# Hybrid attention block on one core: new costs in the planner's table, one probability tile for two heads, and two small products in float32r with stacked parts

## The chip, the cores and the metric

The kernel runs on one core of a Trainium2 chip. The metric is the device time of one execution in microseconds. A core has five engines with instruction streams of their own: TensorE (PE, its weight loads are PEld), VectorE (DVE), ScalarE (ACT), GpSimd (POOL) and SyncE (SP, which only issues transfers here). Each engine works off its stream in order, and waits at an instruction until the semaphores that this instruction needs have come.

## The reference, cut to what matters

One decoder layer over 512 tokens of width 1024, all in float32.

```python
h = rmsnorm(x, norm1_w)
proj = h @ w_in        # columns: A (q, k, v), B (q, k, v, r, low-rank gate a), C (q, k, v)
y_a = dilated_attention(...)   # 6 heads, three (window, dilation) branches, T5 bias
y_b = gla(...)                 # 4 heads, gated linear attention
y_c = moba_attention(...)      # 6 heads, T5 bias; with 512 tokens: causal attention
x = x + concat(y_a, y_b, y_c) @ w_out
x = x + square(relu(rmsnorm(x, norm2_w) @ w_ff1)) @ w_ff2
return rmsnorm(x, final_norm_w)

# in gla, the product that the change touches:
log_a = log_sigmoid(a_lr @ w_a2 + b_a) / 16      # a_lr (512, 16), w_a2 (16, 128)
# in both attentions, the table that the change touches:
bias = rel_bias[rel_bucket(distance)]            # rel_bias (32 buckets, 12 heads)
```

## The kernel before, in words

The large products run in float32r, a reduced form of float32 that TensorE takes in one pass. So that nothing is lost, each factor is split in two parts: `hi`, the rounded value, and `lo`, what the rounding left over. A product is then three matmuls, hi·hi, lo·hi and hi·lo, and the splits are the main work of the other engines: ACT writes `wh` (hi of a weight tile), DVE writes `wl` (the tile less `wh`). Weights come by 512 KB transfers (`wraw`) that SP issues; sums of weight quarters, for a Strassen-like scheme with seven products instead of eight, are added by transfers that POOL issues or by DVE.

The order of the program on PE: the first projection (`first`, tiles `av`, `bq`, `bk`: eight steps of 18 matmuls, one per 128 rows of x); the q and k projections of head pairs 0 and 1 (`qkps`); the v projections (`vps`); `qkps` of pairs 2 to 5; the output projection (`ops`); and four times the two feed-forward products (`f1X`, `f1Y`, `f1Z`, then `f2X`, `f2Y`, `f2Z`). Into these streams of large matmuls small groups are dropped: the row sums `rsp`, the row scale spread over the partitions `rps`, the bias table `vt`, the gate product `zps` and the transposes before it `alps`, the gated attention's level products `lp`, the scores `sps`, transposes of probabilities `ptp`, products with values `po`, and the transposes `yps` before the feed-forward part.

No order is written out by hand. The kernel is a set of generators ("streams", `spawn`) that yield operations and waits. `Plan.run` keeps a clock for each engine and, for each tile, the time at which it is ready; at each step it issues the operation that could start first by these clocks. A cost for every operation stands in `Op.__init__` (lines 39 to 82), and `Plan.issue` adds for a transfer when it will have landed. So a number in that table moves instructions on every engine, and the built order is fixed once the kernel is compiled; the chip's own durations don't change it.

Names that the change and the steps below touch:

- `load_small` (line 622): POOL issues nine small loads: `cst` (identity and masks), `smask`, `hsel`, `rb` (the 32 bucket biases and two rows of ones, 34 rows by 12 heads), `bav`, `wa2` (16 by 128), the two halves of `oneh` (34 by 320, minus one at each distance's bucket), then `lmask` and `gw`. `rb`, `wa2` and `gw` lie in one tile, `misc`.
- `bias_table` (line 665): `vt` = `rb` times `oneh`, two float32 products, copied to `vals` and written to `tab` in DRAM, from where `nb` is read.
- `gla` (line 769): four columns `alr` on DVE, transposes `alps`, copy `alT`, the float32 product `zps` = `wa2` times `alT`, then the gate. `levels` makes seven pairs of factors `kq`; PE multiplies them two levels at a time into four banks (`lp`), and `copy_predicated` on DVE masks them into `attn`. The banks of a group of `lp` come free when its last four masked copies have run.
- `row_scale` (line 635): `rsp`, `ss`, `rstd`, the diagonal `diag` on DVE, then `rps` on PE and from it `R`.
- `attention` (line 951): for each head pair, four masked score groups; the probabilities of each head lie in `P0`, `P1`, `P2`.
- `y_out`, `y_parts`: the second norm, `yps`, `yf`, sums `ys`, and their parts `yp`, which `f1X`, `f1Y`, `f1Z` multiply.

In the profile every operation has line 133, the helper that issues it; in the changed kernel that line is 139. So instructions are told apart by their tiles.

## Time and profile before

| | |
|---|---|
| median of three runs | 565.54 us (564.97 to 566.04) |
| the profiled execution's own time | 565.34 us |
| its span, first to last instruction | 563.5 us |
| PE busy | 554.7 us, 98% of the span |
| PEld busy | 478.4 us, 85% |
| DVE busy | 480.4 us, 85% |
| ACT busy | 370.7 us, 66% |
| POOL busy | 69.7 us, 12% |
| granted TensorE clock | 0.998 |

The profiled execution's time holds the span and 1.8 us around it. A row of the timeline reads: start, duration, engine, line, operation, output<-inputs, shape, count, and in brackets the idle time before it and what ended that. Matmuls are pipelined: a 128x512 one has a duration of about 0.39 us, but the next begins 0.227 us after it. So what a matmul costs the engine is read from the distance of starts, not from its duration, and a busy PE can still lose time between starts.

### The profile page before, as it was taken

The page shows a single profiled execution, that of the slowest core. Times are in us where ns is not written, and L with a number is a line of the kernel's source. Part 1 is how long each engine was busy: PE and PEld are TensorE (multiplying, and loading weights), DVE is VectorE, ACT ScalarE, POOL GpSimd, SP SyncE. Part 2 cuts the span into 40 slices and gives each one's busy share as a digit, 9 for nine tenths or more (in the row PEclk, how much of TensorE's full clock was granted, in tenths as well). Part 3 has the DMA queues.
Part 4 walks back from the last instruction along what each step waited for, and adds up shares of the span by engine and source line. Part 5 has one row for each costly group of instructions (what it writes and reads, how often), then busy time and mean ns, then how long its engine had stood idle before and what let it go on. Part 6 is the DMA issues. An engine that isn't in the chain of part 4 may idle for free.

```text
span 563.5 us, 9460 instructions
## 1 busy us (share of the span) xinstructions
PE 554.7 (98%) x3513; PEld 478.4 (85%) x3513; DVE 480.4 (85%) x875; ACT 370.7 (66%) x658; POOL 69.7 (12%) x91
## 2 busy tenths in 40 slices
PE   9999999999999999999999999999999999999995
PEld 8978887867876768899987899988999888999884
DVE  7799999977868988999699995799957799867985
ACT  8664655884865775989766476855477654579553
POOL 5031110010000002110111010120020110011203
PEclk9999999999999999999999999999999999999999
DMA  8954685585124775992989429687378594395803
GB/s 317 393 123 123 128 217 124 161 335 103 38 43 127 242 150 115 271 272 60 274 212 204 163 64 278 201 151 204 113 158 283 121 201 158 95 220 113 150 12 137
DMA packets 29948, 96.58 MB, mean 171 GB/s; under 512 B 3648, under 2 KB 3690, under 8 KB 29904
## 3 DMA queue, kind: packets, MB, share of 16 engines
q0 software_dynamic: 9456, 33.53, 32.8%
q1 hardware_dynamic: 20160, 62.20, 31.5%
q8 instruction: 27, 0.44, 0.3%
q10 hardware_dynamic: 288, 0.27, 0.1%
q14 instruction: 17, 0.14, 0.1%
HBM read 93.86 MB, written 2.13 MB: 170 GB/s over the span
## 4 chain that ended last, share of the span: by engine, by line
PE 83%; DVE 11%; ACT 2%; issue 2%; DMA 2%; ACTq 0%; POOLq 0%
PE f2X L133 14%; PE f1X L133 13%; PE qkps L133 11%; PE f1Z L133 8%; PE ops L133 7%; PE f2Z L133 7%; PE f1Y L133 4%; PE vps L133 3%; PE f2Y L133 3%; DVE wl L133 3%; PE po L133 2%; PE ptp L133 2%; PE sps L133 2%; PE av L133 2%; DMA wraw<-in_w 2%
## 5 line engine op out<-in xcount | busy, mean ns | idle before, releaser
L133 DVE TENSOR_TENSOR wl<-wraw,wh 128x1024 fp32r<-128x1024 f32 (+2 forms) x174 | 192.0, 1111 | 38.2 <-ACT wh L133 37.2
L133 ACT ACTIVATE wh<-wraw 128x1024 fp32r<-128x1024 f32 (+2 forms) x173 | 164.7, 966 | 58.9 <-DMA wraw<-in_w 10.5
L133 PE MATMUL f1X<-yp,wh 128*128 128x256 f32 x512 | 92.7, 283 | 0.0
L133 PEld LDWEIGHTS f1X<-yp,wh 128*128 128x128 f32 x512 | 80.1, 192 | 0.3
L133 POOL DMA_DIRECT2D wraw<-in_w x46 | 40.8, 962 | 270.3 <-DVE wl L133 219.0
L133 PE MATMUL f1X<-yp,wl 128*128 128x256 f32 x256 | 72.5, 283 | 0.0
L133 PE MATMUL f2X<-wh,Al 128*128 128x512 f32 (+1 forms) x132 | 50.5, 383 | 0.0
L133 PE MATMUL f2X<-wh,Ah 128*128 128x512 f32 (+1 forms) x132 | 50.5, 383 | 0.0
L133 PE MATMUL f2X<-wl,Ah 128*128 128x512 f32 (+1 forms) x132 | 50.5, 383 | 0.0
L133 PEld LDWEIGHTS f1X<-yp,wl 128*128 128x128 f32 x256 | 49.1, 192 | 0.2 <-DVE wl L133 0.2
L133 PE MATMUL f1Z<-yp,wh 128*128 128x256 f32 x256 | 46.3, 283 | 0.0
L133 ACT ACTIVATE h<-h 128x512 f32<-128x512 f32 x56 | 34.7, 625 | 10.3 <-DVE h L133 9.8
L133 PE MATMUL qkps<-xh,wh 128*128 128x512 f32 x96 | 40.1, 417 | 0.0
L133 PEld LDWEIGHTS f1Z<-yp,wh 128*128 128x128 f32 x256 | 39.9, 192 | 0.0
L133 ACT ACTIVATE Ah<-h 128x512 fp32r<-128x512 f32 x40 | 24.0, 620 | 21.5 <-DVE h L133 21.5
L133 PE MATMUL qkps<-xh,wl 128*128 128x512 f32 x96 | 37.5, 391 | 0.0
L133 PE MATMUL qkps<-xl,wh 128*128 128x512 f32 x96 | 37.5, 390 | 0.0
L133 ACT ACTIVATE P<-P,mn 128x512 f32<-128x512 f32 (+3 forms) x48 | 26.6, 555 | 16.6 <-DVE mn L133 16.5
L133 PE MATMUL f1Z<-yp,wl 128*128 128x256 f32 x128 | 36.2, 283 | 0.0
L133 DVE TENSOR_TENSOR Al<-h,Ah 128x512 fp32r<-128x512 f32 x40 | 26.9, 687 | 3.2 <-ACT Ah L133 3.1
L133 PEld LDWEIGHTS f2X<-wl,Ah 128*128 128x128 f32 x132 | 24.8, 188 | 4.9
L133 PEld LDWEIGHTS f2X<-wh,Ah 128*128 128x128 f32 x132 | 24.8, 188 | 4.8
(266 smaller groups left out, 1223.9 us busy)
## 6 DMA issues: line engine op xcount, KB each, us to landing
wraw<-in_w SPq DMA_DIRECT2D x66, 512.0 KB, 5.2
wraw<-in_w POOLq DMA_DIRECT2D x46, 512.0 KB, 6.7
wraw<-in_wqk SPq DMA_DIRECT2D x12, 512.0 KB, 6.1
wraw<-in_wv SPq DMA_DIRECT2D x10, 512.0 KB, 8.6
wraw<-in_wv POOLq DMA_DIRECT2D x8, 512.0 KB, 6.0
wraw<-in_wo SPq DMA_DIRECT2D x8, 512.0 KB, 7.2
wraw<-in_wo POOLq DMA_DIRECT2D x8, 512.0 KB, 5.9
nb<-tab SPq DMA_DIRECT2D x12, 256.0 KB, 4.3
```

The lines of the kernel that those rows point to most:

```text
L133: getattr(getattr(self.nc, op.eng), op.method)(*op.args, **op.kw)
```

## The change

Four things are edited.

1. The planner's table: the 32-row `lp` matmul 0.031 to 0.0635 us; `tensor_tensor_scan` 1.13; `copy_predicated` 0.58 where the last dimension is one, else 0.33; 0.055 more for DVE operations with a per-partition scalar operand and for `scalar_tensor_tensor`. A plain load issued by POOL is now taken to land 3.0 us plus its size over 80 GB/s after its issue, and no longer goes through the clocks of the hardware queue.
2. The probabilities `P2` of the two heads of a pair share one 128x2x256 tile, one buffer instead of two.
3. The bias table: `oneh` and the weights are float32r now. The weights are stacked in 96 rows: rounded biases and the mask rows in rows 0 to 34, zeros, and in rows 64 to 95 the biases' rest; `oneh` repeats its bucket rows there. `rb` is loaded with 96 rows, and `stacked` makes the parts: ACT rounds into `stat`, DVE writes the rest.
4. The gate: `wa2` is loaded three times over (48 rows), with rows 32 to 47 turned into the rest; `alr` is split by three DVE operations into `al3` (rounded, rest, and the unrounded value, which the float32r write rounds), transposed as 48 columns, and `zps` is one float32r product.

```diff
@@ Op.__init__
-                self.cost = 0.031
+                self.cost = 0.0635
...
             self.cost = 0.075 + n * rate / 1000
+            if method == "tensor_tensor_scan":
+                self.cost = 1.13
+            elif method == "copy_predicated":
+                self.cost = 0.58 if args[0].shape[-1] == 1 else 0.33
+            elif any(a.shape[-1] == 1 and n > 4 for a in inner) or method == "scalar_tensor_tensor":
+                self.cost += 0.055
@@ Plan.issue
+            elif op.eng == "gpsimd":
+                end += 3.0 + op.size / 80e3
@@ tiles
-    rb, wa2, gw = misc[:, 0:128], misc[:, 128:256], misc[:, 256:512]
+    rb, wa2, gw = misc[:, 0:16], misc[:, 128:256], misc[:, 256:512]
+    stat = slot("stat", F32R)
+    rbs, wa2s = stat[:, 0:128], stat[:, 128:256]
-    oneh = [slot("oneh", shape=(128, 320)) for _ in range(2)]
-    alT = slot("alT", shape=(128, 512))
+    oneh = [slot("oneh", F32R, (128, 320)) for _ in range(2)]
+    alT = slot("alT", F32R, (128, 512))
@@ load_small
-        for t, d in ((cst, cst_d[:, 0:512]), (smask, cst_d[:, 512:1024]), (hsel, cst_d[:, 1024:1028]), (rb[:34, :12], rb_d),
-                     (bav, ba_d), (wa2[:16], wa2_d)):
+        for t, d in ((cst, cst_d[:, 0:512]), (smask, cst_d[:, 512:1024]), (hsel, cst_d[:, 1024:1028]), (rb[:96, :12], rb_d),
+                     (bav, ba_d), (wa2[:48], wa2_d)):
             yield POOL.dma_start(t, d)
         for i in range(2):
-            yield POOL.dma_start(oneh[i][:34], oh_d[:, i * 320:(i + 1) * 320])
+            yield POOL.dma_start(oneh[i][:96], oh_d[:, i * 320:(i + 1) * 320])
         fire("consts")
+        spawn(stacked(), 1)
         spawn(bias_table(oneh), 1)
...
+    def stacked():
+
+        yield ACT.activation(rbs[:96, :12], rb[:96, :12], AF.Copy)
+        yield DVE.tensor_tensor(rbs[64:96, :12], rb[64:96, :12], f32(rbs[64:96, :12]), op=OP.subtract)
+        yield ACT.activation(wa2s[:48], wa2[:48], AF.Copy)
+        yield DVE.tensor_tensor(wa2s[32:48], wa2[32:48], f32(wa2s[32:48]), op=OP.subtract)
+        fire("stacked")
@@ bias_table
         yield ("wait", "R")
+        yield ("wait", "stacked")
...
-            yield PE.matmul(vt[:, :320], rb, oneh[i], start=True, stop=True)
+            yield PE.matmul(vt[:, :320], rbs, oneh[i], start=True, stop=True)
@@ gla
+        al3 = sp.tile([128, NT, 48], F32R, name="al3", tag="al3", bufs=1)
...
+        yield DVE.tensor_copy(al3[:, :, 0:16], alr)
+        yield DVE.tensor_tensor(al3[:, :, 16:32], alr, f32(al3[:, :, 0:16]), op=OP.subtract)
+        yield DVE.tensor_copy(al3[:, :, 32:48], alr)
...
-        yield [PE.transpose(alps[:16, t * 128:(t + 1) * 128], alr[:, t, :], ident) for t in range(NT)]
-        yield DVE.tensor_copy(alT[:16], alps[:16, :])
+        yield [PE.transpose(alps[:48, t * 128:(t + 1) * 128], f32(al3[:, t, :]), ident) for t in range(NT)]
+        yield DVE.tensor_copy(alT[:48], alps[:48, :])
...
-        yield PE.matmul(zps, wa2, alT, start=True, stop=True)
+        yield PE.matmul(zps, wa2s, alT, start=True, stop=True)
@@ attention
+            A2 = slot("P2", shape=(128, 2, 256))
             for e in range(2):
-                A0, A1, A2 = slot("P0"), slot("P1"), slot("P2", shape=(128, 256))
-                P.append([A1[:, 384:512], A2[:, 0:256], A1[:, 0:384], A0[:, 0:512]])
+                A0, A1 = slot("P0"), slot("P1")
+                P.append([A1[:, 384:512], A2[:, e], A1[:, 0:384], A0[:, 0:512]])
```

Since the planner's numbers change, the order changes on all engines. Three places matter below.

**ACT and PE in the first projection.** On ACT before, from the scaled rows of x (`xh`, `sq`) and weight parts (`wh`) of steps 4 to 6:

```order
L133 ACTIVATE wh<-wraw 128x528
L133 ACTIVATE xh<-xT,nw 128x512
L133 ACTIVATE sq<-xT 128x512
L133 ACTIVATE wh<-wraw 128x528
L133 ACTIVATE xh<-xT,nw 128x512
L133 ACTIVATE sq<-xT 128x512
L133 ACTIVATE wh<-wraw 128x528
```

On ACT now, from the same `wh` on:

```order
L139 ACTIVATE wh<-wraw 128x528
L139 ACTIVATE xh<-xT,nw 128x512
L139 ACTIVATE sq<-xT 128x512
L139 ACTIVATE wh<-wraw 128x528
L139 ACTIVATE stat<-misc 96x12
L139 ACTIVATE xh<-xT,nw 128x512
L139 ACTIVATE wh<-wraw 128x528
L139 ACTIVATE stat<-misc 48x128
L139 ACTIVATE sq<-xT 128x512
```

The two roundings of `stacked` stand between the steps 4 and 5; the first waits for the load of `rb`, the second for that of `wa2`. DVE's two subtractions stand at the same steps. On PE, at the end of the first projection, `rps` before and now:

```order
L133 MATMUL bq<-xh,wl 128x512
L133 MATMUL bk<-xh,wl 128x512
L133 MATMUL rps<-diag,ones 128x512
L133 MATMUL qkps<-xh,wh 128x512
L133 MATMUL qkps<-xl,wh 128x512
```

```order
L139 MATMUL bk<-xh,wl 128x512
L139 MATMUL qkps<-xh,wh 128x512
L139 MATMUL qkps<-xl,wh 128x512
L139 MATMUL qkps<-xh,wl 128x512
L139 MATMUL rps<-diag,ones 128x512
L139 MATMUL qkps<-xh,wh 128x512
```

Three matmuls of the q projection have moved ahead of `rps`. Between the last load part of the first projection and `diag`, DVE now does six `xs` sums of 128x256, three `wl` and one `xsl`; before, four `xs` and two `wl`.

**DVE at the masked copies after the third group of `lp`** (`attn`, one tile for each head; 64x4 and 128x2 are the levels with rows of four and of two). Before:

```order
L133 COPY_PREDICATED attn_615<-lmask,lp 128x64x4
L133 COPY_PREDICATED attn_616<-lmask,lp 128x64x4
L133 COPY_PREDICATED attn_613<-lmask,lp 128x128x2
L133 COPY_PREDICATED attn_614<-lmask,lp 128x128x2
L133 TENSOR_TENSOR wl<-wraw,wh 128x1024 x2
L133 COPY_PREDICATED attn_615<-lmask,lp 128x128x2
L133 COPY_PREDICATED attn_616<-lmask,lp 128x128x2
```

Now:

```order
L139 COPY_PREDICATED attn_638<-lmask,lp 128x64x4
L139 COPY_PREDICATED attn_639<-lmask,lp 128x64x4
L139 COPY_PREDICATED attn_636<-lmask,lp 128x128x2
L139 COPY_PREDICATED attn_637<-lmask,lp 128x128x2
L139 COPY_PREDICATED attn_638<-lmask,lp 128x128x2
L139 COPY_PREDICATED attn_639<-lmask,lp 128x128x2
L139 TENSOR_TENSOR wl<-wraw,wh 128x1024
```

The two `wl` have moved out from between the copies. On PE 24 matmuls `vps` stood between the third and the fourth group of `lp`; now 12 stand there.

**DVE at the entry of the feed-forward part**, where the last transposes `yps` are taken over. Before:

```order
L133 TENSOR_TENSOR yf<-yps,nw_72 128x2x128 x2
L133 TENSOR_TENSOR ys<-yf 128x512 x2
L133 TENSOR_TENSOR wl<-wraw,wh 128x512
L133 TENSOR_TENSOR yp<-ys,yp 128x512
L133 TENSOR_TENSOR h<-h,f1Y 128x512
L133 TENSOR_TENSOR yp<-ys,yp 128x512
L133 TENSOR_TENSOR ys<-ys,yf 128x512
```

Now:

```order
L139 TENSOR_TENSOR yf<-yps,nw_72 128x2x128 x2
L139 TENSOR_TENSOR wl<-wraw,wh 128x512
L139 TENSOR_TENSOR ys<-yf 128x512
L139 TENSOR_TENSOR h<-h,f1Y 128x512
L139 TENSOR_TENSOR ys<-yf 128x512
L139 TENSOR_TENSOR yp<-ys,yp 128x512
L139 TENSOR_TENSOR h<-h,f1Y 128x512
L139 TENSOR_TENSOR yp<-ys,yp 128x512
L139 TENSOR_TENSOR ys<-ys,yf 128x512
```

Both sums into `h`, which read what `f1Y` made, now stand ahead of the second `yp`. On PE the last group of `yps` stood after 42 matmuls `f1X` and now stands after 48 `f1X` and 6 `f1Y`. The parts `wl` of the feed-forward part's fifth product (the one that POOL's last addition waits for) have moved ahead: in DVE's stream three `wl` follow on the sum `h<-h,f1X` where one did, and one `wl` stands ahead of that sum where four did.

## The prediction, made before the changed kernel ran

> **What bounds the kernel now.** First I read the page's busy line and the chain of waits, then the busy time by stage, then what PE waited for.

> ```profile
> PE 554.7 (98%) x3513; PEld 478.4 (85%) x3513; DVE 480.4 (85%) x875; ACT 370.7 (66%) x658; POOL 69.7 (12%) x91
> PE 83%; DVE 11%; ACT 2%; issue 2%; DMA 2%; ACTq 0%; POOLq 0%
> 80.00:100.00 20.00, 19.84 (x123) 15.38 (x122) 20.00 (x41) 10.90 (x17) 1.75 (x2) 1.00 0.56 143
> 300.00:340.00 40.00, 40.00 (x251) 36.26 (x250) 38.70 (x44) 24.32 (x32) 4.40 (x5) 1.00 0.55 143
> 361.86 5.47 PE f2X L133 x24
> PE f2Z L133 <- ACT wh L133: 0.4, 1, 0.4
> PE sps L133 <- DVE mn L133: 0.2, 1, 0.2
> PE lp L133 <- DVE attn L133: 0.2, 1, 0.2
> PE ptp L133 <- DVE rz L133: 0.2, 1, 0.2
> ```

> PE is busy 98% of the span and holds 83% of the chain. In the window rows the first number is the stretch, the next five the busy times of PE, PEld, DVE, ACT and POOL, then the granted clock (1.00). From 300 us on PE has no gap: 24 matmuls `f2X` take 5.47 us, 0.228 each. The second half can gain nothing without fewer matmuls, and the change removes none there. What can move is work of the small float32 groups, and PE's few waits: four named ones of 0.2 to 0.4 us, and one at `zps` seen below. DVE is full from 80 to 100 us (20.00 of 20.00), so the order of its work decides where PE waits next.

> **The change part by part.**

> *The float32 products.* A float32 matmul takes more passes. What one costs is read from starts, since the next matmul takes part of the delay:

> ```profile
> 33.67 0.39 PE L133 MATMUL qkps<-xh,wl 128*128 128x512 f32 x1
> 33.90 0.70 PE L133 MATMUL vt<-oneh,misc 128*128 128x320 f32 x2
> 34.68 0.40 PE L133 MATMUL qkps<-xl,wh 128*128 128x512 f32 x1
> 35.58 0.70 PE L133 MATMUL vt<-oneh,misc 128*128 128x320 f32 x2
> 36.35 0.40 PE L133 MATMUL qkps<-xl,wh 128*128 128x512 f32 x1
> 38.63 0.39 PE L133 MATMUL qkps<-xh,wl 128*128 128x512 f32 x1
> 39.15 1.12 PE L133 MATMUL zps<-alT,misc 128*128 128x512 f32 x2
> 40.35 0.39 PE L133 MATMUL qkps<-xl,wh 128*128 128x512 f32 x1
> ```

> From `vt` to the second matmul behind it: 34.68 − 33.90 = 0.78, and 36.35 − 35.58 = 0.77, each with one `qkps` of 0.23 in it, so 0.55 and 0.54 for `vt`. `zps`: it could start at 38.63 + 0.23 = 38.86, and 40.35 − 38.86 − 0.23 = 1.26, with 0.29 (39.15 − 38.86) of it a wait for `alT`. One float32r pass of 512 columns takes 0.227, so 320 columns about 0.145. The gains are 0.40, 0.40 less about 0.10 at the second (it stands behind transposes, whose switch stays) and 1.03: **−1.73**. The 0.29 goes only if `alT` comes in time: one `vt` and six `qkps`, 1.5 us, now stand between the transposes and `zps`, and a copy of 512 columns takes DVE about 0.6, so I take it as gone. If not, −1.44. The wider transposes (48 columns for 16) change only the weight load, which lies beside other loads: nothing. But the transposes themselves now wait for `al3`, at the end of a dense stretch of DVE work; this is summed up with the next term.

> *The new wait on ACT.* The order has `stat` from `rb` ahead of the `xh` that ACT began at 12.19:

> ```profile
> 9.30 0.57 POOL L133 DMA_DIRECT2D misc<-in_rb  x1
> misc<-in_rb POOLq DMA_DIRECT2D x1, 1.6 KB, 5.7
> lmask<-in_lm POOLq DMA_DIRECT2D x1, 224.0 KB, 6.8
> 12.19 0.71 ACT L133 ACTIVATE xh<-xT,nw 128x512 fp32r<-128x512 f32 x1
> 13.68 0.74 DVE L133 SCALAR_TENSOR_TENSOR xl<-xT,nw,xh 128x512 fp32r<-128x512 f32 x1
> 24.17 0.16 DVE L133 TENSOR_SCALAR ss<-rsp 128x4 f32<-128x4 f32 x1 [3.57 <-PE rsp L133]
> 27.77 0.87 DVE L133 TENSOR_SCALAR diag<-cst,rstd 128x128 f32<-128x128 f32 x4
> 13.68:28.56 14.88, 14.88 (x97) 13.60 (x97) 10.93 (x26) 9.77 (x17) 1.13 (x2) 1.00 1.04 393
> 25.47 0.48 DVE L133 SCALAR_TENSOR_TENSOR xs<-xT,nw,xs 128x256 f32<-128x256 f32 x1
> 28.91 1.02 PE L133 MATMUL rps<-diag,ones 128*128 128x512 f32 x2
> ```

> The load was issued at 9.30 and took 5.7 us to land: 15.0. ACT therefore stands still for about 15.0 − 12.19 = 2.8 us, with six `xh`, `wh` and `sq` of the next steps queued behind it; DVE stops at its own `stat` until about 15.3, 1.6 us after 13.68. The products of those steps are due on PE from 19 us on, so PE does not notice at once. DVE does: between 13.68 and 28.56 it is busy 10.93 us and idle 3.57 of the rest, before `ss`. Now it also has, ahead of `diag`, two more `xs` (0.39 each between starts), one more `wl` and one `xsl` (1.14 each) and two small `stat` (0.15 each): 10.93 + 0.78 + 2.28 + 0.3 = 14.3. From 15.3 that ends at 29.6, and with some 0.6 of dependent small steps (0.34 of idle before) at 30.2 to 30.4. PE, with three more `qkps` ahead of `rps`, reaches it at 28.91 + 3 × 0.23 = 29.6. The stall is **+0.8**. Bounds: 0 if the load lands before ACT arrives, 1.9 if it takes 6.8 us as `lmask`'s did (the late load adds its lateness one for one). Behind `diag` DVE has two `wl`, `Rn`, eight `xs`, `xsl`, one more `wl` and the small `alr` and `al3`, 9.4 us by the durations named, so `al3` is ready at about 39.8; PE reaches the transposes 39 `qkps` behind `rps`, at 30.4 + 0.46 + 8.85 = 39.7. A tie; I take **+0.15**, bounds 0 and 0.6 (one `wl` or `q` late).

> [...]

> *The masked copies of the fourth level group.*

> ```profile
> 76.57 2.64 DVE L133 COPY_PREDICATED attn<-lmask,lp 128x256 f32<-128x256 int32 x6 [0.68 <-PE lp L133]
> 79.02 2.38 DVE L133 TENSOR_TENSOR wl<-wraw,wh 128x1024 fp32r<-128x1024 f32 x2
> 81.31 1.30 DVE L133 COPY_PREDICATED attn<-lmask,lp 128x256 f32<-128x256 int32 x2
> 76.48 0.50 PE L133 MATMUL vps<-wh,xsh 128*128 128x512 f32 x1
> 76.82 0.40 PE L133 MATMUL vps<-wh,xsl 128*128 128x512 f32 x1
> 82.15 0.44 PE L133 MATMUL lp<-kq 32*128 32x64 f32 x6
> 82.75 1.07 PE L133 MATMUL lp<-kq 32*128 32x64 f32 x26 [0.17 <-DVE attn L133]
> ```

> The fourth `lp` waits for the last of eight masked copies. Before, two `wl` (81.31 − 79.02 = 2.29) lay between them, and PE lost 82.75 − 82.15 − 6 × 0.03 = 0.42. Now the eight run straight: six took 79.02 − 76.57 = 2.45, two took 1.30 to their end, so the last ends at 80.3, with 0.15 until PE sees it 80.5, 4.0 us after the third `lp` made way at 76.48. PE has 12 `vps` there, 12 × 0.227 + 0.11 (76.82 − 76.48 is 0.34 where 0.23 is usual) = 2.8, and about 0.15 to switch and for the first six: the stall is 1.0, **+0.55** more than before. The cover is short since the table's new 0.33 for rows of two is under the 0.65 a piece of the last two. Bounds −0.42 (no stall) and +1.1.

> *The feed-forward entry.*

> ```profile
> 253.65 10.09 PE f1Z L133 x84
> 253.82 0.68 DVE L133 TENSOR_TENSOR h<-h,f1Y 128x512 f32<-128x512 f32 x1
> 256.83 0.69 DVE L133 TENSOR_TENSOR yp<-yf,yp 128x512 fp32r<-128x512 f32 x1
> ```

> A matmul `f1Z` takes 0.12 (10.09 over 84). Its sixth factor, the `yp` at 256.83, is due 48 matmuls in, at 253.65 + 5.77 = 259.4, and was there at 257.5. Now the second `h`, which needs the last of `f1Y` (253.65), stands ahead of the second `yp`, so DVE starts again only there, with ten operations up to and with this `yp`: `h`, `yp`, two `ys`, two `yf`, three `wl`, `yp`, at 0.60 each (four `wl` take 2.49 below): 253.7 + 6.0 + 0.1 of tail = 259.8, **+0.45**. Bounds 0 and 2.5 (should DVE reach the second `h` late, since the last `yps` is 12 matmuls, 1.45 us, later, and one `wl` wait too, 0.6).

> *The fifth product's parts.*

> ```profile
> 266.18 2.49 DVE L133 TENSOR_TENSOR wl<-wraw,wh 128x512 fp32r<-128x512 f32 x4
> 267.40 9.03 DMA wraw<-in_w
> 276.51 0.63 ACT L133 ACTIVATE wh<-wraw 128x512 fp32r<-128x512 f32 x1 [2.10 <-DMA wraw<-in_w]
> ```

> POOL's last addition waits for these `wl`; it takes 9.03 us, ACT idles 2.10 for it, and PE pays 0.4 at `f2Z` (0.57 by starts) and 0.2 a little earlier, at 279. The `wl` that releases it now stands some nine or ten operations of 0.60 earlier in DVE's order, about 5.8 us, more than the 2.10, so both stalls go: **−0.77**, bounds −0.77 and 0. What is late next is nothing: behind it the stretch from 300 us is gapless.

> *The attention stage.* The 0.055 more for scalar operands, the scans and the copies with single columns make the planner's DVE clock truer where DVE is full. The waits at `sps` and `ptp` (0.37 and 0.32 by starts) are what is to be won; I take half, **−0.35**, bounds −0.7 and +0.7. Six more visits of PE to small groups at 0.1 each would be 0.6, but most stand where a switch was before; I take one, **+0.1**. DVE has three `al3` and two `stat` more (some 0.8 us) and passes four normalisations of `P` to ACT. The shared `P2` tile takes no engine time: the two heads of a pair used their tiles in the same order before. The `oneh` loads triple in rows and land behind `rb` well before `vt` at 33.9: nothing. Two of the `nb` loads now stand ahead of one more `wqk` on SP's queue, both due tens of us later: nothing.

> The sum: −1.73 + 0.8 + 0.15 + 0.55 + 0.45 − 0.77 − 0.35 + 0.1 = **−0.8**. The profiled execution took 565.34 us (a span of 563.5 and 1.8 around it, which the change leaves alone), 0.2 under the median of 565.54. 565.34 − 0.8 = 564.54; against the median, **564.7**.

> **The rivals.**

> *No wait on ACT.* If `rb` lands within 2.9 us of its issue (12.19 − 9.30), `diag` is ready before PE arrives: 0.8 less, 563.9. Against it: 5.7 in the row, and the other small loads of this stretch between 5.2 and 6.8.

> *The truer clock removes more.* Both attention waits go whole (0.35 more), the cover at `lp` suffices (0.97 less, since the old wait goes too): −0.8 − 1.32 = −2.1, 563.4. For it: the changed costs are just those of this stage's operations. Against it: twelve matmuls, 2.8 us, against 4.0 of copies.

> *Slower: the bias load comes late.* The load now has 96 rows instead of 34, in a stretch where the transfer engines are full (share 1.04 in the window row), and every engine but PE stops behind it. Each us beyond 15.0 is a us at `rps`. It decides from 0.8 + 1.13 = 1.9 us later, a landing at 16.9, 7.6 us after issue; at 17.5 the kernel takes 567.2. Against it: none of POOL's loads took over 6.8.

> *Nothing in sum.* The new order loses elsewhere what the float32 passes gave: with no gain in the attention stage (+0.35) and the waits at `f2Z` and 279 still there (+0.77), the time is 565.8. For it: `f2Z`'s wait hangs on a 9 us transfer, not on DVE alone.

> **How the numbers follow.** What a measurement of this kernel can tell from no change is about 0.2%, 1.13 us: faster means under 564.4, slower over 566.7. Forecast 0.46, own range 564.0 to 565.4; it sits near the bound, so 0.17 of it counts as faster and 0.29 as same. No wait 0.12 and the truer clock 0.15, both faster. Nothing in sum 0.11, same. Slower 0.16. So faster 0.44, same 0.40, slower 0.16. The range goes from a little under the truer clock's 563.4 to the bound of slower: 563.0 to 566.7; it leaves out the late load and a gain of over 2.5.

> **What the changed profile would show.** `vt` as single rows with the next start 0.15 after, `zps` one row with 0.23: the first term. ACT idle 2.8 us before `stat`, ended by the load of `rb`, and PE waiting for DVE's `diag` by 0.8: the second; a wait of 0 there is the first rival, one above 2.9 the third. `lp` waiting for `attn` by 1.0, `f1Z` for `yp` by about 0.5, and no wait of `f2Z` for `wh`: the next three. I would be wrong above all if PE shows a wait over 1 us at a place not named here, or if span and PE's start-to-start losses don't move together.

## The result and the profile after

The changed kernel takes 569.76 us (median of 6 runs, 568.69 to 570.64), the kernel before 565.72 in the same runs: a ratio of 1.0069, 95% interval 1.0059 to 1.0079. It is slower by 4 us, where 0.8 us faster was predicted and 566.7 was the upper end of the range. The profiled execution has a span of 567.8 us, 4.3 more than before.

What PE waited for in the changed kernel (us in total, times, longest):

```profile
span 567.8 us, 9459 instructions
...
PE ptp L139 <- DVE oB L139: 2.7, 1, 2.7
...
PE rps L139 <- DVE diag L139: 0.5, 1, 0.5
PE f1Z L139 <- DVE yp L139: 0.2, 1, 0.2
PE lp L139 <- DVE attn L139: 0.2, 1, 0.2
```

The waits at `sps`, the old one at `ptp` and that at `f2Z` are gone, and `rps` and `f1Z` wait where that was predicted. New, and foreseen by none of the cases, is 2.7 us at `ptp`; a wait of over 1 us at a place not named was the first sign by which the prediction said that it would be wrong. The timeline of DVE and PE around it:

```profile
105.83 0.16 DVE L139 RECIPROCAL rz<-z 128x1 f32<-128x1 f32 x1
110.42 0.23 DVE L139 TENSOR_SCALAR sg<-v 128x128 f32<-128x128 f32 x1 [4.43 <-PE op L139]
113.15 0.68 DVE L139 TENSOR_TENSOR oB<-op,dv 128x512 f32<-128x512 f32 x1
...
109.73 0.65 PE L139 MATMUL op<-s2m,eq 128*128 128x256 f32 x2
110.22 1.00 PE L139 MATMUL op<-vB,attn 128*128 128x64 f32 x8
113.89 1.11 PE L139 MATMUL ptp<-cst,P 128*128 128x128 f32 x4 [2.67 <-DVE oB L139]
115.22 0.63 PE L139 MATMUL vps<-wh,xl 128*128 128x512 f32 x1
115.65 0.63 PE L139 MATMUL vps<-wl,xh 128*128 128x512 f32 x1
119.37 0.40 PE L139 MATMUL vps<-wl,xh 128*128 128x512 f32 x1
119.60 0.39 PE L139 MATMUL vps<-wh,xh 128*128 128x512 f32 x1
```

DVE, full in this stage before, stands still for 4.43 us at `sg`, the gate's input of row blocks 2 and 3, until PE has done the products `op<-s2m,eq`. `sg` does not read anything of these. It only writes, and where it writes the tile `eq` lay. In the built program `sg` gets the slot of `eq` two instructions after the last `op` matmul that reads `eq`. ACT stands still in the same way, 4.26 us before `y`, which got the slot of one of the tiles `attn`. The scores behind `sg` on DVE, and `oB`, which frees the bank that `ptp` needs, come late, and PE stands still 2.67 us. Behind the gap a 128x512 matmul takes 0.43 us (115.22 to 115.65), where 0.23 is usual (119.37 to 119.60). The windows show why (stretch, then the busy times of PE, PEld, DVE, ACT and POOL, granted clock, DMA share, GB/s):

```profile
112.00:114.00 2.00, 0.11 (x1) 0.12 (x2) 2.00 (x11) 2.00 (x8) 0.00 (x0) 0.59 1.04 325
114.00:116.00 2.00, 2.00 (x7) 1.79 (x8) 2.00 (x11) 2.00 (x7) 0.00 (x0) 0.50 0.99 401
116.00:118.00 2.00, 2.00 (x8) 1.52 (x7) 2.00 (x4) 1.55 (x3) 0.00 (x0) 0.50 1.03 422
118.00:120.00 2.00, 2.00 (x9) 1.77 (x9) 2.00 (x3) 1.53 (x4) 0.00 (x0) 0.70 1.03 418
```

The granted clock fell to 0.50 in the gap, at 112.4 us, only 1.2 us after PE's last `op` had ended (110.22 + 1.00), and came back only at 119.2.

Counted by the starts of PE's matmuls against what each form usually takes, the 4.3 us of the two spans go here:

| place | us |
|---|---|
| `rps`, 28.91 + three `qkps` before, 31.23 now | +1.6 |
| transposes that wait for `al3` | +0.2 |
| float32 passes and the wait at `zps` | −1.9 |
| second and fourth `lp` group, less small gains up to 111 us | +0.5 |
| the gap at `ptp` (2.9) and the half clock behind it (2.6) | +5.5 |
| the kernel before's own losses at `sps`, `ptp` and between them, 104 to 132 us | −1.3 |
| 132 to 240 us | −0.2 |
| `f1X` and `f1Z` +0.8, the stalls at 279 us and `f2Z` −0.9 | −0.1 |

The float32 products answer to the prediction's rows:

```profile
41.55 0.39 PE L139 MATMUL vt<-oneh,stat 128*128 128x320 f32 x1
41.78 0.39 PE L139 MATMUL qkps<-xh,wh 128*128 128x512 f32 x1
...
43.14 0.39 PE L139 MATMUL zps<-alT,stat 128*128 128x512 f32 x1
43.37 0.30 PE L139 MATMUL vt<-oneh,stat 128*128 128x320 f32 x1
43.51 0.40 PE L139 MATMUL qkps<-xh,wh 128*128 128x512 f32 x1
```

`vt` now takes 0.23 and 0.14, `zps` 0.23 with no wait, against 0.55, 0.54 and 1.26; each is a single matmul in the rows now (x1), where it was two (x2). But what these products need, the wait at `rps` and the one for `al3`, costs 1.6 + 0.2 of the 1.9 that they save, so by starts the two products earned next to nothing in this kernel.

### The profile page after: what moved, and what is told of

Its sections match the earlier page's. It is cut to its first block, busy times and chain, and to the rows that moved or that the text cites. A ratio compares the mean times of both kernels' runs of the same rounds, so it can differ in the third digit from the quotient of the medians.

```text
span 567.8 us, 9459 instructions
## 1 busy us (share of the span) xinstructions
PE 556.1 (98%) x3510; PEld 480.8 (85%) x3510; DVE 480.2 (85%) x873; ACT 374.0 (66%) x667; POOL 69.6 (12%) x91
## 4 chain that ended last, share of the span: by engine, by line
PE 87%; DVE 5%; ACT 4%; DMA 2%; issue 1%; POOL 0%; SPq 0%; ACTq 0%; DVEq 0%
PE f1X L139 16%; PE f2X L139 15%; PE qkps L139 12%; PE f2Z L139 8%; PE f1Z L139 7%; PE ops L139 6%; PE vps L139 6%; PE f1Y L139 4%; PE f2Y L139 4%; PE ptp L139 3%; PE sps L139 2%; PE po L139 2%; DMA misc<-in_rb 1%; ACT wh L139 1%; PE lp L139 1%
```

## The experiments

The theory (A): the new order puts `op` late, behind the softmax of two head pairs: in the profile 48 of the 144 score matmuls `sps` run before `op`, where 18 did (a pair has 24). The planner keeps no account of the 52 slots in which nearly all 2 KB tiles lie: its clocks know engines, banks, weight buffers and when a tile is ready, not whether a slot is free:

```python
plan = Plan(nc, dict(BANKS, raw=3, rawv=5, rawo=8, w=WPAIRS, big=BIGS, raw2=3, part=5, lev=4, xp=2))
```

Until `op` has run, the gated attention's tiles (`attn`, `eq`, `m`, `s2m`, `vB`) hold their slots. In the built program `op` stands at instruction 1016 to 1054 in the kernel before, and nine slots are free when `sg` takes one; in the changed kernel it stands at 1136 to 1163, no slot is free at 1140, and each tile that comes next gets one that `op` has just read. The main rival (B) was that the stacked products and their wait on `rb` are to blame.

### The old table, the rest of the change kept

```diff
-                self.cost = 0.0635
+                self.cost = 0.031
...
-            if method == "tensor_tensor_scan":
-                self.cost = 1.13
-            elif method == "copy_predicated":
-                self.cost = 0.58 if args[0].shape[-1] == 1 else 0.33
-            elif any(a.shape[-1] == 1 and n > 4 for a in inner) or method == "scalar_tensor_tensor":
-                self.cost += 0.055
...
-            elif op.eng == "gpsimd":
-                end += 3.0 + op.size / 80e3
```

> The changed kernel with the planner's old table; the stacked float32r products and the shared P2 tile stay. Theory A (the 5.4 us at 111 to 119 us come from the new table's order, in which the gated attention's op group stands behind two pairs' softmax and no slot is free before it): here op stands early, no tile takes a slot that op still reads, so the gap at PE and the halved clock behind it are gone: old 565.7 less 1.9 for the float32 passes plus 0 to 0.8 for the wait on rb, 564.0 to 564.6. Rival B (the stacked products, their wait on rb and the denser DVE work are the cause): 568 to 570.

Measured: 568.3 us, ratio 1.0048 (1.0031 to 1.0065). Theory A's number was missed: the time lies where rival B put it, but the loss is another one than that of the changed kernel. There is no gap at 111 us (`op` stands at 1004), and PE waits elsewhere:

```profile
64.71 1.04 PE L133 MATMUL ktp<-hsel,qk 128*128 128x4 f32 x8
67.02 0.50 PE L133 MATMUL vps<-wh,xh 128*128 128x512 f32 x1 [1.27 <-ACT dg L133]
...
67.90 0.63 PE L133 MATMUL vps<-wh,xh 128*128 128x512 f32 x1
...
68.00:69.00 1.00, 1.00 (x4) 0.81 (x3) 1.00 (x4) 0.00 (x0) 0.00 (x0) 0.50 0.51 205
...
200.71 0.41 PE L133 MATMUL ptp<-cst,P 128*128 128x128 f32 x2 [1.40 <-ACT th L133]
```

The half clock is here too: behind a gap of only 1.27 us the granted clock was 0.50 from 67.7 to 71.1 us. So the same table gives another order as soon as the work is a little different, and this order has stalls of its own: these two waits and the slow clock behind the first. The old table is no safe ground to go back to.

### The new table and the shared tile, without the stacked products

The kernel before with the new costs and this:

```diff
+            A2 = slot("P2", shape=(128, 2, 256))
             for e in range(2):
-                A0, A1, A2 = slot("P0"), slot("P1"), slot("P2", shape=(128, 256))
-                P.append([A1[:, 384:512], A2[:, 0:256], A1[:, 0:384], A0[:, 0:512]])
+                A0, A1 = slot("P0"), slot("P1")
+                P.append([A1[:, 384:512], A2[:, e], A1[:, 0:384], A0[:, 0:512]])
```

> The kernel before with the new table and the shared P2 tile alone; the two small products stay in float32. Theory A: DVE stands still at sg behind PE's op, as in the changed kernel, PE then waits 2.5 to 3 us at ptp and runs some 5 us at half clock: 569 to 571. Rival B: no such gap, 565 to 566.

Measured: 568.76 us, ratio 1.0059 (1.0044 to 1.0074), a shade under the range named. The stall is there to the hundredth:

```profile
110.37 0.23 DVE L139 TENSOR_SCALAR sg<-v 128x128 f32<-128x128 f32 x1 [4.43 <-PE op L139]
```

PE waits 2.7 us for `oB`, and the granted clock is 0.50 behind it, as in the changed kernel. The stacked products have no part in it. Nor is this kernel, which leaves them out, slower than the changed one (568.76 for 569.76, with overlapping intervals of the ratios), though its clock was low for 3.4 us and not for 6.8. The new table needs the shared tile: in a program built with the new table and a `P2` for each head, a slot is given away while the tile in it is still to be read. That one was not run.

### Head pair 1 held until `op`

```diff
         yield ops
+        fire("gop")
         for i in range(2):
...
         for p in range(6):
+            if p == 1:
+                yield ("wait", "gop")
             nb = []
```

> The changed kernel, in which head pair 1 of the attention starts only once op has been issued; nothing else is edited. Theory A: op comes earlier in the program, its slots come free before another tile needs them, DVE does not stand still there: 569.8 less 5.4, 564.0 to 565.0. Rival C (the stage's DVE work is simply in a worse order, wherever the slots are): over 567.

Measured: 565.31 us, ratio 0.9991 (0.9982 to 1.0000). The window that held the gap:

```profile
100.00:120.00 20.00, 20.00 (x129) 16.85 (x128) 16.93 (x44) 14.61 (x29) 0.00 (x0) 1.00 0.61 216
```

PE is busy for all of the 20 us, against 17.33 in the changed kernel, and the clock is 1.00. Holding back one pair takes 4.4 us off, to 0.3 above the range named. All other parts of the change, with the new table's costs, are still in.

### Only `sg` moved behind `op`

```diff
         yield ("prio", 2)
+        if t >= 2:
+            yield ("wait", "gop")
         yield DVE.tensor_scalar(sg, v[:, 384:], -1.0, 80.0, op0=OP.mult, op1=OP.min)
```

> The changed kernel, in which the gate's sg of row blocks 2 and 3 is issued only after op. Theory A (the pool of slots is empty, so whatever tile comes next gets a slot that op reads; here it would be P1 of pair 1, which takes the slot of s2m): DVE stands still some 4 us all the same, 569 to 570. Rival A2 (the fault is only where sg stands): the gap goes, 564 to 565.

Measured: 568.41 us, ratio 1.0051 (1.0033 to 1.0069): under the 569 to 570 of theory A, far over the rival's 565. The next tile takes the place of `sg`:

```profile
110.56 0.56 DVE L139 CUSTOM_DVE_ANT_0 P<-sps,nb 128x384 f32<-128x384 f32 x1 [3.31 <-PE op L139]
...
116.00:118.00 2.00, 2.00 (x9) 1.48 (x8) 1.25 (x7) 1.52 (x5) 0.00 (x0) 0.50 1.03 416
```

It is `P1` of pair 1, which took the slot of `s2m`. So it is not the place of one instruction; the pool of slots was empty. PE's wait fell into two parts, 1.67 and 0.99 us, and the clock still fell to 0.50, for 3.4 us where it was 6.8.

### The roundings of `rb` behind the row scale

The kernel of the third experiment with

```diff
     def stacked():
 
+        yield ("wait", "rstd")
```

> The kernel of e3 (pair 1 held until op is issued), in which the roundings of rb and wa2 wait for the row scale rstd in the planner, so that they stand behind rps on ACT and DVE. Theory of the rb wait (ACT stands still 2 to 3.6 us at stat in the first projection, DVE eats its reserve, PE loses 0.4 to 1.25 us at rps): ACT and PE do not wait there, and the time is 0.4 to 0.8 under e3's 565.3, 564.5 to 564.9. Rival (rps would be late anyway by the xs, wl and xsl that now stand ahead of diag): the same as e3, and PE still waits for diag.

Measured: 565.12 us, ratio 0.9988 (0.9978 to 0.9998): not to be told from the third experiment's 0.9991. ACT does not wait at `stat` and PE not at `rps`, as theory said. But PE pays at the second level group:

```profile
30.26 1.02 PE L139 MATMUL rps<-diag,ones 128*128 128x512 f32 x2
...
66.06 1.99 PE L139 MATMUL lp<-kq 32*128 32x64 f32 x58 [0.66 <-ACT attn L139]
```

PE reaches this group 0.73 us earlier than in the third experiment (64.96 for 65.69), of which 0.50 is there already at the last `bk` of the first projection (29.33 for 29.83; put down to the difference at the start that the last section describes), but it can go on only 0.33 earlier (66.06 for 66.39): ACT's copies for `attn` came hardly earlier. So part of what is won at `rps` is given back here.

How the wait itself works is told by five runs whose order is the same in this stretch. The start of `stat` on ACT and of `rps` on PE were 15.12 and 30.85 us in the third experiment, 15.50 and 31.23 in the changed kernel, and

```profile
15.84 0.21 ACT L139 ACTIVATE stat<-misc 96x12 fp32r<-96x12 f32 x1 [2.23 <-DMA misc<-in_rb]
31.57 1.10 PE L139 MATMUL rps<-diag,ones 128*128 128x512 f32 x2 [1.27 <-DVE diag L139]
```

in the run with 22 spare matmuls below; with two more of this order, each time 15.72 or 15.73 lie between them. The load's lateness goes to `rps` one for one.

### Without the landing rule for POOL's loads

```diff
-            elif op.eng == "gpsimd":
-                end += 3.0 + op.size / 80e3
```

> The changed kernel without the one rule of the table that lets a load by POOL land 3.0 us plus its size over 80 GB/s after its issue; all the rest stays. Theory A: here op stands earlier and no tile soon takes a slot that op reads, so the gap at 111 us and the slow clock behind it are gone, though every new DVE and PE cost is in: 564 to 565.5. Rival (the new DVE costs themselves make the order bad): over 567.

Measured: 565.32 us, ratio 0.9990 (0.9978 to 1.0001). All costs of DVE and PE are the new ones, and no gap: `op` stands at 1097, and no tile takes a slot that `op` reads within 40 instructions. What this order waits for:

```profile
PE ptp L139 <- ACT th L139: 1.6, 2, 1.3
...
PE ops L139 <- DVE x L139: 1.0, 1, 1.0
PE lp L139 <- DVE attn L139: 0.7, 1, 0.7
```

A rule that prices twelve transfers by POOL (the small loads, of which there are ten, not nine, in the first 16 us, and the two writes of `tab`) decides, by the order that grows from it, whether 5 us are lost at 111.

### The shared tile alone

The kernel before with the diff of the second experiment and nothing else.

> The kernel before with the shared P2 tile alone. The planner does not know the slots, so the order is the same to the instruction; only which slot a tile gets is different. Theory A: op is early here and slots are plenty, so 565.7, no change within 0.2%. Rival (one tile for two heads ties the second head to the first and costs DVE or PE time): over 566.9.

Measured: 567.19 us, ratio 1.0025 (1.0014 to 1.0035). Not a large loss, but clear of no change, and in the rival's range. What was expected of the order was wrong: it is not that of before. The planner doesn't know the slots, but it keeps its ready times by tile, so with one `P2` a step of one head also waits, in its clocks, for what the other head writes. In the profile DVE has 872 instructions for 875 and ACT 661 for 658, since three normalisations of `P` went to ACT, and PE's order is another from about 108 us on. By starts PE loses 1.4 us more between 132 and 242 us, in waits of 0.2 to 0.5 at `ptp` and `ops`:

```profile
PE ops L133 <- DVE x L133: 0.3, 1, 0.3
...
PE ptp L133 <- ACT th L133: 0.2, 1, 0.2
PE ptp L133 <- ACT P L133: 0.2, 1, 0.2
```

Tiles behind the first `P2` get other slots too. How much of the 1.4 us is the order's and how much the slots' was not told apart.

### The masked copy at its measured cost

In the changed kernel's profile the four masked copies with rows of two stand 0.53, 0.58 and 0.58 us apart (79.09 to 80.79), where the table has 0.33. The kernel of the fifth experiment with

```diff
-                self.cost = 0.58 if args[0].shape[-1] == 1 else 0.33
+                self.cost = 0.58 if args[0].shape[-1] == 1 else 0.53 if args[0].shape[-1] == 2 else 0.33
```

> The kernel of e5 with the planner's cost of a masked copy with rows of two at 0.53 us, as measured, instead of 0.33. Theory of the fourth level group (PE loses 0.8 us at it since the planner thinks the copies done too early): the loss there goes to 0.4 or less, and the time is 0.4 under e5, 564.2 to 564.5. Rival (another order brings another wait of the same size): the same as e5 or slower.

Measured: 563.56 us, ratio 0.9961 (0.9949 to 0.9974), the fastest kernel here, under the kernel before and under the fifth experiment's 565.12, and under the range named as well. PE does not wait at the fourth group any more: from its first start to the next large matmul the group takes 1.05 us, where it took 2.26 in the fifth experiment. That is 1.2 of the 1.6 us; the rest is the new order's and was not followed up. What is left:

```profile
PE ptp L139 <- DVE rz L139: 0.8, 1, 0.8
PE lp L139 <- ACT attn L139: 0.7, 1, 0.7
PE f1Z L139 <- DVE yp L139: 0.3, 1, 0.3
```

### PE kept at work in the gap

The changed kernel, with matmuls that do nothing behind `op` (they write to an unused half of a bank):

```diff
+        for _ in range(22):
+            x = PE.matmul(st["spare"][:, 256:512], xl[0][:, :128], xh[0][:, :256], start=True, stop=True, skip_group_check=True)
+            x.cost, x.outs = 0.0, []
+            ops.append(x)
         yield ops
```

> The changed kernel, order the same to the instruction, with 22 spare matmuls of 256 columns (0.12 us each, 2.6 us in all, results unused) on PE behind op, where PE stands still for 2.7 us. They do nothing but keep PE at work; the wait of ptp for DVE stays. Theory of the clock (of the 5.4 us lost at 111 to 119 us, 2.7 are the wait, and 2.5 the half clock that follows from the idle time): no row at a clock of 0.50 behind the gap, 569.8 less 2.5, some 567.3. Rival (the clock falls for another reason, such as the load on the chip, or the slow matmuls wait for data): 569 to 570.5.

Measured: 569.84 us, ratio 1.0071 (1.0055 to 1.0086), a miss. The clock did stay:

```profile
116.88 0.39 PE L139 MATMUL vps<-wl,xh 128*128 128x512 f32 x1
117.11 0.40 PE L139 MATMUL vps<-wh,xh 128*128 128x512 f32 x1
...
114.32 0.42 DVE L139 CUSTOM_DVE_ANT_0 P<-sps,nb 128x256 f32<-128x256 f32 x1 [1.49 <-PE sps L139]
```

A matmul takes 0.23 us right behind the gap (116.88 to 117.11). But a score on DVE that reads the other half of that bank now waited 1.49 us for the spare matmuls, and with it `oB` and `ptp`. `rb` landed late besides (the row in the fifth experiment). So the run was made again with fewer:

```diff
-        for _ in range(22):
+        for _ in range(10):
```

> As e9, with 10 spare matmuls instead of 22 (1.2 us, so that they end before DVE's last masked score needs PE's count, which in e9 held DVE for 1.5 us more). Theory of the clock: ptp starts as late as in the changed kernel, PE is idle for some 1.5 us instead of 2.7, the clock stays at 1.00, and the time is 569.8 less 2.5, 567.0 to 567.8. Rival (the spare matmuls change nothing at the end, since PE waits for DVE work that is late anyway): 569 to 570.

```profile
114.21 0.63 PE L139 MATMUL ptp<-cst,P 128*128 128x128 f32 x4 [1.67 <-DVE oB L139]
...
112.00:114.00 2.00, 0.54 (x5) 0.33 (x3) 1.95 (x11) 2.00 (x8) 0.00 (x0) 1.00 1.06 355
114.00:116.00 2.00, 1.79 (x10) 1.44 (x10) 2.00 (x11) 2.00 (x7) 0.00 (x0) 1.00 0.98 401
```

Measured: 568.06 us, ratio 1.0045 (1.0031 to 1.0058), 1.7 under the changed kernel's 569.76, and 0.3 above the range named. `ptp` starts about as late (114.21 for 113.89), PE is idle 1.67 us, and the clock stays at 1.00. So the half clock alone cost some 1.7 us of the median, not 2.5: with PE fast again, three `ptp` groups wait for about 0.3 each, which the slow clock may have covered.

### The float32 passes alone

The kernel of the eighth experiment, order the same, with the two products read as float32 (`priced` only keeps the planner's cost as it was):

```diff
-            yield PE.matmul(vt[:, :320], rbs, oneh[i], start=True, stop=True)
+            yield priced(PE.matmul(vt[:, :320], f32(rbs), f32(oneh[i]), start=True, stop=True), 320)
...
-        yield PE.matmul(zps, wa2s, alT, start=True, stop=True)
+        yield priced(PE.matmul(zps, f32(wa2s), f32(alT), start=True, stop=True), 512)
```

> The kernel of e8, order the same to the instruction, with vt and zps read as float32 again, so that only the passes on PE come back. By the starts in the trace of before vt costs 0.55 and 0.54 and zps 0.97 without its wait, by those of the changed kernel 0.23, 0.14 and 0.23: the time is e8's 563.6 plus 1.3 to 1.5, about 565.0. Rival (PE's time there is hidden by a wait of later work for DVE): under 564.2.

Measured: 564.83 us, ratio 0.9988 (0.9979 to 0.9996), 1.27 us over the eighth experiment, or 1.5 by the two ratios to the kernel before. In an order without the gap the passes are worth what the starts say (1.3 to 1.5).

### Without the landing rule, the masked copy at its measured cost

The sixth experiment's kernel with the cost line of the eighth.

> The kernel of e6 (no rule for POOL's landing) with the masked copy with rows of two at 0.53 us. Theory of the fourth level group: its loss of 1.02 us in e6 falls under 0.4, and the time is 564.5 to 565. Rival (a new order brings waits of its own; op stands later here than in e6, but no tile soon takes a slot that it reads): 565 to 567.

Measured: 566.24 us, ratio 1.0006 (0.9997 to 1.0016). The rival was right: the fourth group loses 0.34 by starts instead of 1.02, but near 195 and 218 us new waits came:

```profile
PE ptp L139 <- ACT th L139: 1.3, 3, 0.8
...
PE ops L139 <- DVE m L139: 1.0, 1, 1.0
PE sps L139 <- DVE mn L139: 0.4, 1, 0.4
```

A truer number took away the loss that it was about and brought others by the order. One thing more can be read from this run: `op` stands at 1154 to 1188 here, later than in the changed kernel, and at 1146 no slot is free, yet DVE waits for `op` only 0.2 us in all (at `oB`, which reads it) and the clock stays at 1.00 (0.997 over the whole execution, for 0.993 in the changed kernel). The first tile that takes a slot of `op`'s comes 35 instructions after the last read, where it is 2 for `sg` in the changed kernel. So a late `op` and an empty pool of slots don't suffice; what costs the time in the changed kernel is the write right behind the read.

## Why the prediction was wrong

**The step that failed** is "the attention stage": "The waits at `sps` and `ptp` [...] are what is to be won; I take half, −0.35, bounds −0.7 and +0.7", argued from a planner's clock made truer. The two waits did go. But that `op` moved behind two pairs of softmax was in the order and was not costed. Its price follows from the rows: DVE 4.43 us behind PE's `op`, PE 2.67 behind DVE, half clock after it: 5.5 us by starts, 4.4 of the median when one edit takes it away (third experiment). The rival "Nothing in sum" did say that the new order loses elsewhere, but put 1.1 us on it, and none of the bounds held this loss. With it gone the kernel is at 565.3: the same as before by the bound of 0.2%.

**"The shared `P2` tile takes no engine time: the two heads of a pair used their tiles in the same order before"** was wrong too, by 1.4 us (seventh experiment). The sentence asked what the tile costs on an engine, not what moves when the planner takes two heads' tiles for one and every tile behind them can get another slot.

**The float32 products** (−1.73): right, 1.9 by starts with the wait at `zps`, 1.27 for the passes alone.

**The wait on ACT** was right in kind and in the stall of ACT (2.8 us predicted, 2.78 in the row below), under-sized at `rps`: 0.8 predicted, 1.6 measured.

```profile
15.50 0.21 ACT L139 ACTIVATE stat<-misc 96x12 fp32r<-96x12 f32 x1 [2.78 <-DMA misc<-in_rb]
...
31.23 1.10 PE L139 MATMUL rps<-diag,ones 128*128 128x512 f32 x2 [0.53 <-DVE diag L139]
```

`rb` was issued 0.4 later and landed near 15.4, not 15.0, and DVE had 0.45 more idle behind it, so `rps` began at 31.23, not 30.4. The waits view shows only 0.5 of it, since PE was itself 0.9 late by then (the last `bk` at 29.61 for 28.68; the last section), which would else have been wait. From issue to landing the load took 5.7 us in the changed kernel too, as in the kernel before, so the rival "No wait on ACT" fell. The rival of a late load fell too: it would have had to land at 16.9. In sum the term matters little, since the fifth experiment takes it away and gains nothing that can be measured.

**The transposes behind `al3`**: 0.15 predicted, 0.18 by starts; the wider ones themselves took 0.27 us each, as the narrow ones did, and their weight loads 0.10 for 0.09. **The fourth level group**: +0.55 predicted, +0.45 measured (it lost 0.8 where it lost 0.34), for the reason given: the cost of rows of two, which the eighth experiment mends. **The feed-forward entry**: +0.45 predicted (its own times, 259.8 less 259.4, give 0.4), 0.56 by starts at `f1Z`, with 0.24 at `f1X` that was not foreseen. **The fifth product's parts**: −0.77 predicted, and both stalls are gone.

**"The truer clock removes more"** had its two attention waits right. Nothing else of it came, and in the changed kernel the truer table brought the largest loss; the sixth, eighth and eleventh experiments say that its entries are not at fault one by one: each re-casts the order, and each order brings waits of its own, at slots or elsewhere.

Which entry of the table puts `op` behind the softmax isn't settled. Without the landing rule it does not stand there, so the rule is needed for it, and the stacked products are not, since it stands there without them. Whether the rule would do it alone, with the old costs, was not run.

## What to carry to other kernels

Where a planner sets the order and a pool hands out the buffers, read from the built program not only what each engine does next but what each tile's buffer held last, and who reads it: a write that needs nothing can wait for a reader on another engine, as `sg` on DVE did here, 4.43 us for PE. A planner that knows its buffers as it knows its banks would have seen an empty pool; until then, look for the point at which the most tiles are alive, see how soon after its last reader a slot is written again, and hold back the stream that only adds to them. And where a planner keeps its times by tile, two tiles made one are a change of the order, even if no work is added. And cost an order that has moved by the instructions that moved farthest, not by the costs that were mended.

## What the runs showed of the hardware

At the start, too, the pace of PE differs from one execution to the next. The matmul `bq` of the first step, in the kernel before and in the seventh experiment, whose order is the same up to 108 us:

```profile
5.32 0.39 PE L133 MATMUL bq<-xh,wh 128*128 128x512 f32 x1
```

```profile
5.97 0.60 PE L133 MATMUL bq<-xh,wh 128*128 128x512 f32 x1
```

In the first, `bk` begins 0.23 us after it (5.55); in the second 0.43 (6.40), the distance seen at the half clock, and from there on 0.24 (6.64). PE is then 0.86 us late (6.64 for 5.78 at the next `av`). The changed kernel's profile has the late kind (`bq` 5.97, `bk` 6.40), the profile of before the early one. The windows give a granted clock of 1.00 from 3 to 7 us for these two; the clock's own records in their traces begin, with 1.00, only at 6.6 us in the changed kernel's and at 4.5 in that of before, where the pace changes. At the second `bq` the two profiles are 0.93 us apart (7.21 and 6.28); single profiles of this kernel can therefore not be compared to better than 0.9 us in sum, and the medians were used for that.
